# Hybrid attention and mLSTM block: x normalised by tokens and turned on TensorE, GpSimd out of the early stage, another order of group 0 and of the modulation

## Chip, cores and metric

One Trainium2 chip, one core. The metric is the device time of one execution in microseconds (us).

## What is computed

One decoder block on x of 512 tokens by 2048 channels, float32. What matters here is its head:

```
mod = c @ w_ada + b_ada
shift, scale, gate = split(mod, 3)
h = rmsnorm(x, norm_gain) * (1 + scale) + shift
proj = h @ w_in
```

`proj` feeds eight attention heads with three dilated windows, four mLSTM heads behind a causal convolution, and gates; two projections, a merge, an output projection, the gated residual and a last RMSNorm follow. All of that is untouched.

## The kernel before

Every product is made of three float32r matmuls: an operand is cast to a high part (`hi`, on ScalarE, ACT), the rest (`lo`) is subtracted (`split`, L170), and hi x hi, hi x lo and lo x hi are summed in PSUM (`mm3`, L273). So each weight costs a cast and a subtraction before TensorE (PE) can use it.

h is needed with channels on partitions, in 16 tiles of 128 channels by 512 tokens; tile k is called h_k here. x is handed in twice, as it is and turned (`xT`); the early stage loads the turned one. `first_norm` squares its 16 tiles, sums them over channels by matmuls with ones and by additions on VectorE (DVE), and gets 1/rms for all 512 tokens on every partition. Tile k is multiplied by it (`normed`, L387), the first on DVE, the others on GpSimd (POOL). `modulated` (L390) then scales and shifts the tile by the modulation of its channels, splits it and stores it to DRAM for later.

The modulation is a product of c with w_ada, done on DVE: for each column of 128 channels two pieces of 1024 values are multiplied with c and summed (`modulation`, L328, the instruction is at L338). A tile of h needs four pieces (scale and shift), 64 in all. Four lists feed the engines: `loads` gives the order of the DMA issues on SyncE's queue (SP), through rings of 8 buffers (`y`, for the pieces), 3 (`raw`) and 1 (`more`); `stream` is the order in which weights are split, three halves ahead of the matmuls (`step`, L254); `pieces` is the modulation, `modulate(n)` brings it to n pieces; `late` holds evacuations. Every engine runs its instructions in the order in which this Python code issues them, and waits by semaphores.

The early stage takes turns k = 0 to 15. Turn k has one weight unit `ws` of two halves (`first_products`: 18 matmuls on h_k, six accumulators kept in PSUM for all turns), and units of the table TURNS (`extra_products`): ten more output columns of 128, whose sums over k are cut in five groups (GROUPS), each group summed in PSUM and then copied (group 0, ACT) or added (L517, DVE) to a tile in SBUF. The pair (g, n) in TURNS stands for group g and the columns n and n+1. 288 + 480 matmuls of 512 columns are the stage. POOL makes `lo` of the `extra` units and of h (except h_0); DVE makes `lo` of `ws`, the pieces and the additions. The modulation is paced by turns: at the start of turn k, 4(k+1) + 2 pieces are asked for, and over the turn four more.

Of the kernel before, what the change touches and what calls it, by code (L numbers as in the profile page):

```python
# [16 lines left out]
P = 128  # L17
# [87 lines left out]
def block_kernel(ctx: ExitStack, tc, xT, x, c, cst, abias, ada, ws, wu, wv, fgain, out):  # L105
# [72 lines left out]
    stream, loads, pieces, ready, late, tasks, beside = [], [], [], [], [], [], []  # L178
    at = {"load": 0, "split": 0, "half": 0, "piece": 0, "raw": 0, "more": 0, "y": 0}
# [9 lines left out]
    def add(u):  # L189
        stream.append(u)  # L190
        loads.append(u)

    def load_ahead():
        while at["load"] < len(loads):
            u = loads[at["load"]]
            if u.ring == "any":
                u.ring = "raw" if at["raw"] < RAW or "more" not in tags else "more"
            if at[u.ring] == {"raw": RAW, "more": MORE, "y": ADA}[u.ring]:
                if u.ring == "more":
                    u.ring = "any"  # L200
                break
            if u.at_load:
                u.at_load()
            u.raw = S(u.ring)
            dma(u.raw[:, : u.width], u.src)
            at["load"] += 1
            at[u.ring] += 1

    def prepare():
# [9 lines left out]
        else:  # L219
# [6 lines left out]
            if later and u.low is None:  # L226
                normed(later.pop(0), nc.gpsimd)
# [67 lines left out]
    def load_x(n):  # L295
        for _ in range(n):
            t = S("gm")
            dma(t, xT[len(xt)])
            xt.append(t)
# [4 lines left out]
    load_x(4)  # L304
# [4 lines left out]
    load_x(12)  # L309
# [8 lines left out]
    nc.vector.tensor_copy(bmod, cs[:, C_BADA : C_BADA + 3 * KD])  # L318
    nc.vector.tensor_scalar(bmod[:, KD : 2 * KD], bmod[:, KD : 2 * KD], 1.0, None, ALU.add)
# [37 lines left out]

    def first_norm():

        acc = S("w")  # L360
        root = const.tile([P, 1], F32, name="root")
        nc.scalar.activation(root, eps, AF.Sqrt)
        ss = PS("m")
        for k in range(KD):
            sq = acc[:, :512] if k == 0 else S("hb")
            nc.scalar.activation(sq, xt[k], AF.Square)
            if k % 3 == 2 and k < KD - 2:
                nc.tensor.matmul(ss, ones, sq, start=k == 2, stop=False)
            elif k:
                nc.vector.tensor_tensor(acc[:, :512], acc[:, :512], sq, ALU.add)  # L370
        nc.tensor.matmul(ss, ones, acc[:, :512], start=False, stop=True)
        rstd = acc[:, 512:]
        nc.scalar.activation(rstd, ss, AF.Sqrt, bias=eps, scale=1.0 / D)
# [7 lines left out]
        for k in range(1, 4):  # L381
            normed(k, nc.gpsimd)

    rs = []
# [4 lines left out]

    def modulated(k):  # L390
        def f():
# [4 lines left out]
            nc.scalar.activation(xt[k], xt[k], AF.Identity, bias=mods[:, k : k + 1], scale=gs)  # L396
# [1131 lines left out]
```

## Time and profile before

| what | us |
|---|---|
| median of 3 runs (1635.78 to 1636.86) | 1635.82 |
| profiled execution | 1637.23 |
| its span | 1635.4 |
| PE busy, share of the span | 1565.2, 96% |
| DVE busy | 1147.9, 70% |
| ACT busy | 704.6, 43% |
| POOL busy | 139.8, 9% |
| chain that ended last | PE 71%, DVE 13%, issue 6%, ACT 4% |

Busy times are unions over an engine's instructions. In the lines of the trace, L is the line of the kernel, `out<-in` names the tiles with their buffer numbers left out, and the name behind `<-` in brackets or after an idle time is what the engine waited for. PEld, the loading of weights, runs beside PE. A matmul's duration contains its way through the array, so that neighbours overlap; the distance of their starts is their price. POOL's 139.8 us lie nearly all in the first seventh of the span.

### The profile page before, as it was taken

The page shows a single profiled execution, that of the slowest core. Times are in us where ns is not written, and L with a number is a line of the kernel's source. Part 1 is how long each engine was busy: PE and PEld are TensorE (multiplying, and loading weights), DVE is VectorE, ACT ScalarE, POOL GpSimd, SP SyncE. Part 2 cuts the span into 40 slices and gives each one's busy share as a digit, 9 for nine tenths or more (in the row PEclk, how much of TensorE's full clock was granted, in tenths as well). Part 3 has the DMA queues.
Part 4 walks back from the last instruction along what each step waited for, and adds up shares of the span by engine and source line. Part 5 has one row for each costly group of instructions (what it writes and reads, how often), then busy time and mean ns, then how long its engine had stood idle before and what let it go on. Part 6 is the DMA issues. An engine that isn't in the chain of part 4 may idle for free.

```text
span 1635.4 us, 24961 instructions
## 1 busy us (share of the span) xinstructions
PE 1565.2 (96%) x9686; PEld 1388.3 (85%) x9686; DVE 1147.9 (70%) x1933; ACT 704.6 (43%) x1189; POOL 139.8 (9%) x112
## 2 busy tenths in 40 slices
PE   3799899999999999999999999999999999999997
PEld 1576689988888888999999999999999788878887
DVE  6788867667746568888788887888896444474445
ACT  3332344335525434455454454454443843343234
POOL 2665540000000000000000000000000000000000
PEclk7999999999999999999999999999999999999999
DMA  8677735665222344344443444444444654432333
GB/s 313 241 276 273 272 113 168 223 217 179 90 94 74 104 163 159 139 152 130 142 144 124 146 145 137 144 142 132 133 161 149 216 176 137 176 105 95 125 117 129
DMA packets 93879, 260.01 MB, mean 159 GB/s; under 512 B 10424, under 2 KB 14648, under 8 KB 93760
## 3 DMA queue, kind: packets, MB, share of 16 engines
q1 hardware_dynamic: 79928, 233.24, 41.6%
q10 hardware_dynamic: 13832, 25.18, 4.4%
q8 instruction: 76, 1.25, 0.3%
q14 instruction: 43, 0.35, 0.1%
HBM read 229.02 MB, written 29.36 MB: 158 GB/s over the span
## 4 chain that ended last, share of the span: by engine, by line
PE 71%; DVE 13%; issue 6%; ACT 4%; DMA 3%; POOL 1%; SPq 0%; ACTq 0%; DVEq 0%; POOLq 0%
PE ps L280 47%; PE ps L807 23%; DVE y L338 3%; DVE lo L173 2%; ACT sh L172 2%; DVE cs L780 1%; DVE e L822 1%; DVE cs L784 1%; DVE cs L785 1%; DMA raw<-ws 1%; DVE sl L173 1%; DVE al L786 1%; DMA p<-kept 1%; DMA more<-ws 1%; ACT gm L396 1%
## 5 line engine op out<-in xcount | busy, mean ns | idle before, releaser
L173 DVE TENSOR_TENSOR lo<-raw,hi 128x512 fp32r<-128x512 f32 (+2 forms) x238 | 177.5, 751 | 172.1 <-ACT hi L172 171.7
L172 ACT CAST hi<-raw 128x512 fp32r<-128x512 f32 (+3 forms) x276 | 161.2, 596 | 277.9 <-PE ps L280 227.4
L807 PE MATMUL ps<-t,sh 128*128 128x256 f32 x1344 | 245.3, 282 | 0.0
L807 PEld LDWEIGHTS ps<-t,sh 128*128 128x128 f32 x1344 | 208.0, 190 | 0.0
L807 PE MATMUL ps<-t,sl 128*128 128x256 f32 x672 | 189.3, 282 | 0.0
L779 ACT CAST ah<-raw 128x768 fp32r<-128x768 f32 x112 | 93.6, 836 | 204.8 <-issue 105.2
L280 PE MATMUL ps<-ha,hi 128*128 128x512 f32 x384 | 126.5, 409 | 26.1 <-ACT ha L172 17.2
L173 DVE TENSOR_TENSOR sl<-cs,sh 128x1024 fp32r<-128x1024 f32 x112 | 137.3, 1226 | 16.0 <-ACT sh L172 15.7
L172 ACT CAST sh<-cs 128x1024 fp32r<-128x1024 f32 x112 | 117.6, 1050 | 67.8 <-DVE cs L785 67.4
L786 DVE TENSOR_TENSOR al<-raw,ah 128x768 fp32r<-128x768 f32 x112 | 106.9, 955 | 52.8 <-ACT ah L779 52.6
L280 PE MATMUL ps<-hi,h 128*128 128x512 f32 (+1 forms) x512 | 143.6, 366 | 0.0
L280 PE MATMUL ps<-hi,ha 128*128 128x258 f32 (+1 forms) x512 | 129.8, 339 | 0.0
L280 PE MATMUL ps<-hi,hb 128*128 128x258 f32 (+1 forms) x512 | 129.3, 339 | 0.0
L807 PEld LDWEIGHTS ps<-t,sl 128*128 128x128 f32 x672 | 127.8, 190 | 0.0
L280 PE MATMUL ps<-hb,hi 128*128 128x512 f32 x384 | 122.0, 397 | 1.6 <-POOL hb L173 1.6
L280 PEld LDWEIGHTS ps<-ha,hi 128*128 128x128 f32 x384 | 73.9, 195 | 48.3 <-ACT ha L172 19.2
L280 PEld LDWEIGHTS ps<-hi,h 128*128 128x128 f32 x512 | 91.8, 188 | 17.0
L807 PE MATMUL ps<-hb,ah 128*128 128x256 f32 x448 | 87.1, 287 | 11.5 <-DVE e L822 9.9
L280 PEld LDWEIGHTS ps<-hi,ha 128*128 128x128 f32 x512 | 87.8, 188 | 11.4 <-issue 0.4
L280 PEld LDWEIGHTS ps<-hi,hb 128*128 128x128 f32 x512 | 87.9, 188 | 10.8
L280 PE MATMUL ps<-lo,h 128*128 128x512 f32 (+1 forms) x256 | 93.9, 367 | 2.4 <-DVE lo L173 2.4
L280 PE MATMUL ps<-h,hi 128*128 128x512 f32 x286 | 89.6, 395 | 0.0
(276 smaller groups left out, 3461.8 us busy)
## 6 DMA issues: line engine op xcount, KB each, us to landing
raw<-wu SPq DMA_DIRECT2D x223, 512.0 KB, 3.6
y<-ada SPq DMA_DIRECT2D x64, 512.0 KB, 7.3
g<-kept SPq DMA_DIRECT2D x56, 256.0 KB, 3.9
kept<-e ACTq DMA_DIRECT2D x56, 256.0 KB, 2.5
raw<-ada SPq DMA_DIRECT2D x24, 512.0 KB, 3.7
more<-wu SPq DMA_DIRECT2D x16, 512.0 KB, 3.5
raw<-wv SPq DMA_DIRECT2D x12, 516.0 KB, 3.7
kept<-g ACTq DMA_DIRECT2D x20, 256.0 KB, 4.2
```

Of the source, the lines that this page charges most:

```text
L172: nc.scalar.copy(hi, src)
L173: (low or nc.vector).tensor_tensor(lo, src, as32(hi), ALU.subtract)
L280: nc.tensor.matmul(ps, a, b, start=first and n == 0, stop=last and n == 2)
L338: nc.vector.tensor_tensor_reduce(out=raw[:, :1024], in0=raw[:, :1024], in1=cb[half][:, :1024], scale=1.0, scalar=bmod[:, col : col + 1] if ...
L396: nc.scalar.activation(xt[k], xt[k], AF.Identity, bias=mods[:, k : k + 1], scale=gs)
L779: nc.scalar.copy(ah, r[:, HT : 4 * HT])
L780: nc.vector.tensor_tensor(two(s[:, : 2 * HT]), two(r[:, HT : 3 * HT]), r[:, :HT].unsqueeze(1).to_broadcast([P, 2, HT]), ALU.add,)
L784: nc.vector.tensor_tensor(s[:, 2 * HT : 3 * HT], s[:, :HT], r[:, 2 * HT : 3 * HT], ALU.add)
L785: nc.vector.tensor_tensor(s[:, 3 * HT :], s[:, 2 * HT : 3 * HT], r[:, 3 * HT : 4 * HT], ALU.add)
L786: nc.vector.tensor_tensor(al, r[:, HT : 4 * HT], as32(ah), ALU.subtract)
L807: nc.tensor.matmul(banks[bank][:, n * HT : (n + 1) * HT], x[:, w], y, start=count[bank] == 1, stop=count[bank] == 24 * len(BANKS[bank]),)
L822: nc.vector.tensor_tensor(v[:, 0:2, :], twice(v[:, 4, :]), two(bb), ALU.add)
```

## The change

- The turned copy of x is no longer handed in. The early stage loads x with tokens on partitions, 16 tiles of 128 tokens by 512 channels. The squares are summed along the row by the squaring instruction itself (10 tiles on ACT, 6 on DVE), so 1/rms is one value per partition. The tiles are scaled in groups of four (`normed`, on ACT; the first group half on DVE), and turned on PE by `turned`: four matmuls with the identity into one PSUM tile, then a copy by ACT (h_0 is read from PSUM). Tiles 0 to 3 are turned at the start, two more after each of the first six `ws`.
- GpSimd makes no `lo` and no scaling any more; DVE makes every `lo`.
- TURNS puts all five units of group 0 into turn 1.
- `loads` is two lists, one for the `y` ring and one for the others.
- The modulation is paced by matmuls: one piece more per 10 matmuls issued, besides 4(k+1) + 2 at the start of turn k.

The core of the diff (left out: the removed input's plumbing and line-for-line renames of the two lists):

```diff
-    1: [(0, 0)], 2: [(0, 2), (0, 4)], 3: [(0, 6)], 4: [(0, 8)],
+    1: [(0, 0), (0, 2), (0, 4), (0, 6), (0, 8)],
...
-            if later and u.low is None:
-                normed(later.pop(0), nc.gpsimd)
...
+    def load_x(j):
+        for t in range(NT):
+            xn[j][t] = S("gm")
+            dma(xn[j][t], x[t * P : (t + 1) * P, j * T : (j + 1) * T])
...
     def first_norm():
+        sums = const.tile([P, NT, NT], F32, name="sums")
+        for j in range(NT):
+            for t in range(NT):
+                to, junk = sums[:, t, j : j + 1], S("hb")
+                if (j * NT + t) % 8 in (2, 5, 7):
+                    nc.vector.tensor_tensor_reduce(
+                        out=junk, in0=xn[j][t], in1=xn[j][t], scale=1.0, scalar=0.0,
+                        op0=ALU.mult, op1=ALU.add, accum_out=to,
+                    )
+                else:
+                    nc.scalar.activation(junk, xn[j][t], AF.Square, accum_out=to)
...
+        nc.vector.tensor_reduce(rstd, sums, mybir.AxisListType.X, ALU.add)
+        nc.scalar.activation(rstd, rstd, AF.Sqrt, bias=eps, scale=1.0 / D)
         nc.vector.reciprocal(rstd, rstd)
-        normed(0, nc.vector)
+        normed(0, True)
+        for k in range(4):
+            turned(k)
         modulate(3)
         for _ in range(2):
             prepare()
         modulate(4)
-        for k in range(1, 4):
-            normed(k, nc.gpsimd)
+        normed(1)
...
+    def normed(j, both=False):
+        for t in range(NT):
+            r = rstd[:, t : t + 1]
+            if both and t % 2:
+                nc.vector.tensor_scalar(xn[j][t], xn[j][t], r, None, ALU.mult)
+            else:
+                nc.scalar.activation(xn[j][t], xn[j][t], AF.Copy, scale=r)
+
+    def turned(k):
+        ps = PS("m")
+        for t in range(NT):
+            nc.tensor.transpose(ps[:, t * P : (t + 1) * P], xn[k // 4][t][:, k % 4 * P : (k % 4 + 1) * P], ident)
+        if k == 0:
+            xt.append(ps)
+        else:
+            xt.append(S("hb" if k < HK else "gm"))
+            nc.scalar.copy(xt[k], ps)
...
-            split(xt[k], a, b, nc.gpsimd if k else None)
+            split(xt[k], a, b)
...
-    AHEAD = 2
-    def next_pieces():
-        k, n, i = turn
-        modulate(4 * (k + 1) + AHEAD + 4 * (i + 1) // n)
-        turn[2] += 1
+    AHEAD, PACE = 2, 10
+    def next_pieces(n):
+        emitted[0] += n
+        modulate(4 + AHEAD + emitted[0] // PACE)
...
     def first_products(k, half):
+            if half == 1 and k < 6:
+                for i in range(2 * k + 4, 2 * k + 6):
+                    turned(i)
+                if k % 2 == 1 and k < 4:
+                    normed(k // 2 + 2)
...
-            next_pieces()
+            next_pieces(9)
...
-                Unit(next(src)[:, :width], width, [extra_products(g, n), extra_products(g, n + 1)], low=nc.gpsimd)
+                Unit(next(src)[:, :width], width, [extra_products(g, n), extra_products(g, n + 1)])
...
-    loads[:5] = loads[1:4] + loads[:1] + loads[4:5]
+    load_ahead("y", 3)
+    load_ahead("raw", 1)
     load_ahead()
```

How the order moves is shown at the end of turn 4 and the start of turn 5. ACT before, from the last cast of group 0 (`gm_103` is h_4, L515 copies products of group 0 out of PSUM, `raw_498` is the `ws` of turn 5):

```order
L172 CAST hi_597<-raw_467 128x256
L396 ACTIVATE gm_103<-gm_103,mods,gs_621 128x512
L172 CAST ha_624<-gm_103 128x512
L162 DMA kept_627<-gm_103 128x512
L172 CAST hi_629<-raw_498 128x384
L172 CAST hi_643<-raw_498 128x384
L515 COPY g_647<-ps_634 128x512
L172 CAST hi_659<-more_539 128x512
L515 COPY g_663<-ps_649 128x512
```

ACT in the change, from the second half of turn 5's `ws` (`raw_531`) to h_5 (`hb_332`); L409 copies turned tiles out of PSUM, `more_566` is the first `extra` unit of turn 5:

```order
L172 CAST hi_711<-raw_531 128x384
L409 COPY gm_729<-ps_724 128x512
L409 COPY gm_736<-ps_731 128x512
L172 CAST hi_740<-more_566 128x512
L420 ACTIVATE hb_332<-hb_332,mods,gs_749 128x512
L172 CAST ha_752<-hb_332 128x512
```

Copies of turned tiles stand where copies of group 0 stood, and they come right before the cast of `hi_740`, with h_5 behind it.

DVE before, at the same place (the ISA rows are pieces of the modulation with the reading of their sums, `gs` is the last scalar before h is made, `gs_717` that of h_5):

```order
L173 TENSOR_TENSOR lo_644<-raw_498,hi_643 128x384
L338 ISA y_614,mods<-y_614,w_134,acc_641 128x1024
L338 ISA mods 128x1
L338 ISA y_616,acc_697<-y_616,w_133,bmod 128x1024
L338 ISA acc_697 128x1
L338 ISA y_618,mods<-y_618,w_134,acc_697 128x1024
L338 ISA mods 128x1
L393 TENSOR_TENSOR gs_717<-mods,cs 128x1
```

DVE in the change, up to h_5 (`gs_749`):

```order
L173 TENSOR_TENSOR lo_712<-raw_531,hi_711 128x384
L173 TENSOR_TENSOR lo_741<-more_566,hi_740 128x512
L340 ISA y_551,acc_744<-y_551,w_132,bmod 128x1024
L340 ISA acc_744 128x1
L340 ISA y_592,mods<-y_592,w_133,acc_744 128x1024
L340 ISA mods 128x1
L414 TENSOR_TENSOR gs_749<-mods,cs 128x1
L173 TENSOR_TENSOR ha_752<-hb_332,ha_752 128x512
```

A `lo` of an `extra` unit (`lo_741`), which POOL made before, stands ahead of the last two pieces of h_5, and the subtraction of h_5 stands behind them.

PE in the change, the end of turn 4's `ws` and the start of turn 5's (L404 turns x, L281 is the product):

```order
L281 MATMUL ps_295<-ha_688,hi_643 128x512 x2
L281 MATMUL ps_295<-ha_688,lo_644 128x512
L404 MATMUL ps_724<-cs,gm_117 128x128
L404 MATMUL ps_724<-cs,gm_119 128x128
L404 MATMUL ps_724<-cs,gm_121 128x128
L404 MATMUL ps_724<-cs,gm_123 128x128
L404 MATMUL ps_731<-cs,gm_117 128x128
L404 MATMUL ps_731<-cs,gm_119 128x128
L404 MATMUL ps_731<-cs,gm_121 128x128
L404 MATMUL ps_731<-cs,gm_123 128x128
L281 MATMUL ps_290<-ha_752,hi_680 128x512 x2
L281 MATMUL ps_290<-ha_752,lo_681 128x512
```

The eight turns stand between the two `ws`; before, PE had two halves of group 0 there, the last unit of that group.

## Rows read from the trace of the kernel before

**Rows 1.** Busy time by stretch: columns are named in the first line.
```profile
core 0: us, PE busy (x) PEld busy (x) DVE busy (x) ACT busy (x) POOL busy (x), PEclk, DMA share, GB/s
10.00:20.00 10.00, 7.12 (x9) 1.68 (x8) 5.99 (x9) 6.34 (x11) 0.00 (x0) 0.87 1.03 401
...
24.55:36.07 11.52, 0.00 (x1) 0.00 (x1) 9.86 (x13) 1.48 (x3) 7.81 (x4) 0.50 0.80 292
...
36.07:105.20 69.13, 57.88 (x213) 43.02 (x213) 56.33 (x71) 24.54 (x49) 39.60 (x26) 0.91 0.70 253
...
246.77:400.00 153.23, 153.23 (x1044) 141.17 (x1043) 102.93 (x209) 61.33 (x114) 0.00 (x0) 1.00 0.61 204
...
200.00:220.00 20.00, 20.00 (x87) 16.18 (x86) 14.94 (x22) 8.96 (x16) 10.14 (x7) 1.00 0.53 193
```

**Rows 2.** Timeline, DVE, one turn: start us, us, engine, line, operation [idle before <-releaser].
```profile
121.33 0.68 DVE L517 TENSOR_TENSOR g<-g,ps 128x512 f32<-128x512 f32 x1
121.94 1.27 DVE L338 CUSTOM_DVE_ANT_0 y<-y,w,bmod 128x1024 f32<-128x1024 f32 x1
...
126.57 1.33 DVE L173 TENSOR_TENSOR lo<-raw,hi 128x384 fp32r<-128x384 f32 x1 [1.95 <-ACT hi L172]
127.83 2.31 DVE L338 CUSTOM_DVE_ANT_0 y<-y,w,bmod 128x1024 f32<-128x1024 f32 x1
...
212.59 0.15 DVE L393 TENSOR_TENSOR gs<-mods,cs 128x1 f32<-128x1 f32 x1
```

**Rows 3.** Groups by line and shape, 0 to 245 us: busy us, mean ns | idle before.
```profile
L338 DVE CUSTOM_DVE_ANT_0 y<-y,w,bmod 128x1024 f32<-128x1024 f32 x32 | 59.2, 1850 | 0.0
...
L338 DVE CUSTOM_DVE_ANT_0 y<-y,w,acc 128x1024 f32<-128x1024 f32 x32 | 47.7, 1489 | 0.7
...
L173 DVE TENSOR_TENSOR lo<-raw,hi 128x384 fp32r<-128x384 f32 x24 | 31.1, 1302 | 22.1 <-ACT hi L172 22.1
```

**Rows 4.** Timeline, the start, up to the first matmuls on h0.
```profile
8.54 8.03 ACT L366 ACTIVATE hb<-gm 128x512 f32<-128x512 f32 x12 [0.74 <-DMA gm<-xT]
...
24.55 2.29 DVE L338 CUSTOM_DVE_ANT_0 y<-y,w,bmod 128x1024 f32<-128x1024 f32 x1
...
34.37 0.15 DVE L393 TENSOR_TENSOR gs<-mods,cs 128x1 f32<-128x1 f32 x1
...
36.05 0.69 DVE L173 TENSOR_TENSOR ha<-gm,ha 128x512 fp32r<-128x512 f32 x1 [1.53 <-ACT ha L172]
...
36.07 1.52 PE L280 MATMUL ps<-ha,hi 128*128 128x512 f32 x2 [16.27 <-ACT ha L172]
...
36.66 0.55 DVE L173 TENSOR_TENSOR lo<-raw,hi 128x384 fp32r<-128x384 f32 x1
```

**Rows 5.** Timeline, PE, the first matmul behind the early stage.
```profile
246.77 0.28 PE L280 MATMUL ps<-hi,ha 128*128 128x258 f32 x1
```

**Rows 6.** Groups by line and shape over the whole span, for prices.
```profile
L173 DVE TENSOR_TENSOR lo<-raw,hi 128x512 fp32r<-128x512 f32 x190 | 129.7, 688 | 129.6 <-ACT hi L172 129.4
...
L515 ACT COPY g<-ps 128x512 f32<-128x512 f32 x10 | 5.8, 582 | 0.9 <-PE ps L280 0.9
...
L1298 ACT ACTIVATE y<-y,fr 128x512 f32<-128x512 f32 x8 | 5.4, 716 | 0.9 <-DVE fr L1294 0.9
...
L982 PE MATMUL ps<-cs,w 128*128 128x128 f32 x32 | 4.8, 272 | 0.0
```

**Rows 7.** Busy time by stretch, after the two gaps of PE.
```profile
54.72:58.00 3.28, 2.99 (x7) 2.02 (x8) 3.28 (x2) 1.95 (x5) 3.28 (x3) 0.53 0.98 317
66.36:76.00 9.64, 9.64 (x42) 7.82 (x42) 8.57 (x11) 3.66 (x8) 6.50 (x5) 1.00 0.80 290
```

**Rows 8.** Timeline, PE, matmuls behind a gap [idle before <-releaser].
```profile
43.97 0.50 PE L280 MATMUL ps<-ha,hi 128*128 128x512 f32 x1 [0.93 <-ACT ha L172]
...
54.72 0.64 PE L280 MATMUL ps<-ha,hi 128*128 128x512 f32 x1 [2.41 <-ACT hi L172]
...
66.36 0.73 PE L280 MATMUL ps<-ha,hi 128*128 128x512 f32 x2 [2.37 <-ACT g L515]
```

More of the change, by code (lines that the diff above doesn't have):

```diff
@@ L104, in block_kernel @@
 @with_exitstack
-def block_kernel(ctx: ExitStack, tc, xT, x, c, cst, abias, ada, ws, wu, wv, fgain, out):
+def block_kernel(ctx: ExitStack, tc, x, c, cst, abias, ada, ws, wu, wv, fgain, out):
     nc = tc.nc
@@ L177, in block_kernel @@
     pos = [0, 0]
-    stream, loads, pieces, ready, late, tasks, beside = [], [], [], [], [], [], []
-    at = {"load": 0, "split": 0, "half": 0, "piece": 0, "raw": 0, "more": 0, "y": 0}
+    stream, loads, pieces, ready, late, tasks, beside = [], {"y": [], "raw": []}, [], [], [], [], []
+    at = {"split": 0, "half": 0, "piece": 0, "raw": 0, "more": 0, "y": 0}
     def begin(*desc):
@@ L190, in add, with load_ahead @@
         stream.append(u)
[L191 to L207, printed above, removed]
+        loads["raw"].append(u)
+    def load_ahead(only=None, most=99):
+        for kind in [only] if only else loads:
+            while loads[kind] and most:
+                u = loads[kind][0]
+                if u.ring == "any":
+                    u.ring = "raw" if at["raw"] < RAW or "more" not in tags else "more"
+                if at[u.ring] == {"raw": RAW, "more": MORE, "y": ADA}[u.ring]:
+                    if u.ring == "more":
+                        u.ring = "any"
+                    break
+                if u.at_load:
+                    u.at_load()
+                u.raw = S(u.ring)
+                dma(u.raw[:, : u.width], u.src)
+                loads[kind].pop(0)
+                at[u.ring] += 1
+                most -= 1
     def prepare():
@@ L293, in block_kernel @@
     begin_part("heads", "left", y=(8, 1032), w=(4, 1024), gm=(17, 512), mk=(1, P))
[L295 to L299, printed above, removed]
+    xn = [[None] * NT for _ in range(NT)]
+    def load_x(j):
+        for t in range(NT):
+            xn[j][t] = S("gm")
+            dma(xn[j][t], x[t * P : (t + 1) * P, j * T : (j + 1) * T])
     crow = [S("g") for _ in range(4)]
@@ L308, in block_kernel @@
     tri = cs[:, C_TRI : C_TRI + P]
-    load_x(12)
+    for j in range(1, NT):
+        load_x(j)
     mask = S("mk")
@@ L348, in modulation @@
             u = Unit(ada[col * 2 + half], use=use(half), at_load=at_load if half == 0 else None, ring=ring)
-            loads.append(u)
+            loads["y" if ring == "y" else "raw"].append(u)
             (pieces if then or ring == "y" else stream).append(u)
@@ L356, in block_kernel @@
     qm, km, szm = [None] * 8, [None] * 8, [None] * 8
+    rstd = const.tile([P, NT], F32, name="rstd")
     def first_norm():
-        acc = S("w")
         root = const.tile([P, 1], F32, name="root")
         nc.scalar.activation(root, eps, AF.Sqrt)
[L363 to L373, printed above, removed]
+        sums = const.tile([P, NT, NT], F32, name="sums")
[9 more added lines that the diff above has]
+                    nc.scalar.activation(junk, xn[j][t], AF.Square, accum_out=to)
+        nc.vector.tensor_copy(bmod, cs[:, C_BADA : C_BADA + 3 * KD])
+        nc.vector.tensor_scalar(bmod[:, KD : 2 * KD], bmod[:, KD : 2 * KD], 1.0, None, ALU.add)
+        nc.vector.tensor_reduce(rstd, sums, mybir.AxisListType.X, ALU.add)
+        nc.scalar.activation(rstd, rstd, AF.Sqrt, bias=eps, scale=1.0 / D)
         nc.vector.reciprocal(rstd, rstd)
-        rs.append(rstd)
-        normed(0, nc.vector)
+        normed(0, True)
+        for k in range(4):
+            turned(k)
         modulate(3)
@@ L395, in f @@
             )
[L396 removed]
+            src = xt[k]
+            if k == 0:
+                xt[0] = S("hb")
+            nc.scalar.activation(xt[k], src, AF.Identity, bias=mods[:, k : k + 1], scale=gs)
             if k < HK:
@@ L443, in f @@
                 modulate(4 * (k + 1) + AHEAD)
-                turn[:] = [k, 2 * (1 + len(TURNS.get(k, []))), 0]
             if k == 0 and half == 0:
@@ L764, in pair_units @@
                 unit = Unit(src, ring="raw")
-                loads.append(unit)
+                loads["raw"].append(unit)
                 paired.append((d, u, unit))
```

19 lines of the change are left out of this document (5 added, 14 removed).

## The prediction

> **What bounds the kernel now.** I read the stretches first [rows 1], then the order of time on VectorE (DVE) in one turn of the early stage [rows 2], then the groups of instructions by line up to 245 us [rows 3]. The reader should see two kernels in one. From 246.8 us on TensorE (PE) is busy without a gap for the next 153 us and nearly so to the end (1565 us of the whole span), and no line of the change touches that part: what the early stage loses or wins, the end loses or wins. The early stage is 768 matmuls of 512 columns (288 `first`, 480 `extra`). Dense, 87 of them take 20 us, 0.230 us each [rows 1], 176.6 us in all; they stand from 36.07 us [rows 4] to 246.77 us [rows 5], 210.7 us, so PE loses 34 us there. From 24.55 [rows 4] to 212.6 us [rows 2] DVE carries the pieces, and until about 193 us it is the bound: in a turn [rows 2] it runs four pieces of the modulation, two `lo` halves and some additions, and stands idle once, 1.95 us, until ScalarE (ACT) has cast the new h. These idles sum to 22.1 us before the larger `lo` group [rows 3], and to 30 with the rest of the 16 turns. PE waits for that chain at each turn's start.
>
> A piece of 1024 columns takes 1.27 us when GpSimd (POOL) is still and up to 2.31 us when it works, 1.67 in the mean of all 64; a `lo` of 384 columns 1.3 in the mean instead of 0.55 [rows 2 to 4]. So GpSimd's help is paid by DVE.
>
> **The change part by part.** The sum is made against the profiled execution, 1637.2 us with a span of 1635.4; the median of the runs is 1635.8, and I move the result down by 1.4 us at the end. A measurement can tell about 0.2%, 3.3 us, from no change.
>
> *GpSimd out.* The 64 pieces go from 106.9 us [rows 3] to 64 x 1.27 = 81: minus 25. Up to the last piece 29 `lo` of 384 go from 1.3 to 0.5: minus 23. DVE takes over 24 `lo` of 512 at 0.61 (their duration is 0.69 [rows 6], but after an addition of 0.68 the next instruction starts 0.61 later [rows 2]), 10 of 256 at about 0.33 (scaled) and 15 of h at 0.61: plus 27. The idle for h becomes 1.53 us, as at the first h, where DVE already did the subtraction [rows 4], minus 6. DVE's own work from the first piece to the last falls from 188 us (24.55 to 212.6) to about 161. That is the gain the change can reach, if DVE never stands idle in a new place.
>
> *Start.* The squares stay paced by x, whose last square ended at 16.57 us [rows 4]. Matmuls of the sum, a root and a reciprocal over 512 columns, 8 us up to the first piece at 24.55 [rows 4], fall away; 16 sums per row and four small instructions (some 0.2 us each) follow, so rstd stands near 17.8. Two scalings on DVE (an estimate of 0.5 each, under the 0.69 of a subtraction with two operands [rows 6]) end at 18.8, three pieces at 22.6. On ACT two scalings (0.7 [rows 6]) end at 19.2; then PE does 16 turns. A turn of 128x128 costs 0.15 us at full clock [rows 6]; PE stands at half clock here [rows 1], so 0.3 and an end at 23.2. Copy, two casts, two `lo`, the fourth piece: 26.7. From gs to the first matmul 1.7 us passes [rows 4]: **28.4 instead of 36.07**, 7.7 us won. Loads: the activations' matrix pieces go ahead of the second ws, which by the rate of the start (some 400 GB/s [rows 1], 1.3 us per 512 KB) lands near 28.7; it is wanted at 31, so the new load order costs nothing, and that margin is its cover. x comes in as many and as large pieces as before. SP's queue keeps its place otherwise: a y load no longer stands behind a raw load that waits, which takes waits away.
>
> *The turns on PE.* 48 more of 0.15 us lie on PE's path: 7 us. More costly is what hangs behind them, in order, on three queues. After each of the first six ws, PE gets two tiles to turn; ACT's next two instructions copy them out; only behind those copies (and after turns 1 and 3 behind four scalings) stands the cast of the next `hi`; DVE's next instruction waits for that cast, and behind it stand the pieces of the next h. Before, the casts that stood behind copies of PSUM were those whose `lo` POOL made; DVE's own `lo` was cast right behind h.
>
> Let E be the end of the 18 matmuls of a ws. Both tiles are turned at E+1.2 and copied at E+1.9 (0.58 a copy [rows 6]), the cast is done at E+2.5, `lo` at E+3.1, two pieces at E+5.6 (a cast of 512 is put at a copy's 0.6), and gs to PE adds 1.7: the next h is there at **E+7.3**; PE has nothing from E+1.2 on. With four scalings in between (2.7 us) but one piece less behind them it is E+8.4. The 18 matmuls take 4.1 us, or 5.7 when the clock starts at half after such a gap; I take the half start where the gap is over 3 us. PE's starts of h0, h1 and so on then are:
> - h1: E0 = 35.4 (18 matmuls took 7.0 at the start [rows 4, 8]); ACT scales the next group first; copies at 37.4, cast 37.8, `lo`, one piece, gs: **41.0** (before 43.97 [rows 8]).
> - Turn 1 holds all 60 matmuls of group 0: 18 + 60 matmuls, 17.9 us, half a clock at the start 1.6, turns 1.2, a stop of 2 us where the copies and scalings stand before the cast of `hi`, and one of 2 us for the two PSUM buffers left: h2 at **65.8**. DVE stands still for some 7 us there.
> - h3 follows at once: **71.3**. h4, with the scalings: E3 = 75.5, **83.9**. h5: E4 = 89.6, **97.0**.
> - Turn 5 has 48 more matmuls that need no new h, but pieces are now due one per 10 matmuls, and 216 matmuls ask for 27 pieces where h6 needs 28: the 28th is only asked for with h6 itself, after the last addition. E5 = 102.7, turns 1.2, 11.0 of matmuls, addition, piece, gs: **118.4**. At this point the kernel before had also done these 216: its records count 213 from 36.07 to 105.20 us [rows 1]. So 13 us behind.
> - Turns 6 to 8 (42 matmuls, 9.7 us): by the same chain (last addition, piece, gs) 13.4, 11.7 and 10.7 us, since the rule by matmuls gets ahead by one or two pieces per turn: h9 at **154.2** with 342 matmuls done.
> - From there DVE (10.7 us for 42 matmuls) and PE (9.7) run abreast and the pieces end early: 426 x 0.230 = 98.0, plus some 2 us for DVE in turns 11 and 12, plus 2 in the last ten halves, where DVE now does `lo`, addition and convolution (0.33 + 0.6 + 0.7 per 1.38 us of PE). End of the stage: **256**, against 246.8: **9 us later**, 1646 for such an execution and **1645** as a median.
>
> Unknown prices: scaling on ACT lies between a copy's 0.58 and, as far above the like row [rows 6], 0.85; I take that row, 0.7. A turn lies between 0.06, a quarter of a dense 512-column matmul, and 0.27, its whole duration [rows 6]; I take the dense 0.15. The two move the end by minus 5 and plus 6 us. The clock: after a gap of 2.41 us the matmuls ran at about half clock for 3.3 us, after one of 2.37 us at full clock [rows 7, 8], each seen once. If it never falls after h0, the end comes 4.5 us sooner; if it falls at every start to h9, 4 later.
>
> The Trainium skill (TensorE: Matmul & The Clock Gate, section Loop structure matters more than you think) holds that long waits between groups of matmuls let the array go cold and the next ones run slow. This case's trace agrees at one of the two gaps and not at the other. By that rule the sum would be the one of a fall at every start, 1649; by the gap that kept its clock, 1640.5.
>
> **The rivals.** *DVE's relief wins.* For it: DVE was idle at no other place than h, so 27 us of work less could come through whole. Then the pieces end at 18.8 + 161.5 + 2 = 182, PE then has some 165 matmuls left after the next `lo` (2.8 us), 38 us, with PE's own work in turn 1 and the tail 4 to 8 more: 229, 18 us sooner, **1618**. It decides if DVE waits for the copies of the turns for less than 1 us per turn. Against it: the cast of `hi` stands behind the copies by the order. The Trainium skill (SBUF — State Buffer, section Who interferes with whom) has a VectorE instruction with two SBUF inputs and a GpSimd instruction that reads SBUF contend for a shared pair of ports. The trace agrees, 1.27 against 2.31 us [rows 2], and this rule alone would give this rival. *Half of it:* waits on ACT and PE overlap better than I add them, and the start's 7.7 us cover them: **1634 to 1639**, no change. *Worse:* the half clock holds through the turns to h6, and DVE's casts miss each turn by an addition more: 10 us on top, **1655**.
>
> **How the numbers follow.** My sum adds many waits in series; an error of 8 us in it is easy, and it can lose more than it can gain. Forecast (9 us slower, itself 1639 to 1651): 0.52; worse: 0.10; no change: 0.13; relief wins, whole or in good part: 0.25. Faster 0.25, same 0.13, slower 0.62. The range leaves out the far half of the relief and of the worse case: **1622 to 1654**.
>
> **What would show it.** Right: the first matmul near 28; DVE idle several us before a `lo` in turns 1 to 5, released by an ACT cast that itself waited for copies of PSUM; PE gaps of 3 to 7 us before h4, h5 and h6; 216 matmuls at about 118 us; pieces of 1.27 us; dense PE from about 155. Wrong: fewer than 15 us of such idles on DVE, or 216 matmuls done by 105 us; then the relief wins.

## The result, and the profile after

The changed kernel takes 1659.77 us (median of 4 runs, 1658.78 to 1660.82), the kernel before in runs on the same chip 1636.34 us: a ratio of 1.0143, 95% interval 1.0125 to 1.016. It is 23.4 us slower. The forecast had the sign, but it said 9 us where the runs show 23, and its range ended at 1654.

| | before | after |
|---|---|---|
| profiled execution, its span | 1637.23, 1635.4 | 1660.09, 1657.8 |
| first matmul on h0 | 36.07 [rows 4] | 28.00 |
| end of the early stage (first 128x258 matmul) | 246.77 [rows 5] | 264.13 |
| from there to the end | 1388.6 | 1393.7 |
| busy: PE, DVE, ACT, POOL | 1565.2, 1147.9, 704.6, 139.8 | 1578.7, 1127.1, 719.0, 17.6 |

PE's timeline after, at the starts of h0, h1 and h4 to h9 and at the end of the stage (columns as in [rows 2], which answers for DVE; the two lines of L404 are the turns behind the 18 matmuls on h4 and on h5):

```profile
28.00 1.52 PE L281 MATMUL ps<-ha,hi 128*128 128x512 f32 x2 [5.00 <-ACT ha L172]
...
40.04 1.52 PE L281 MATMUL ps<-ha,hi 128*128 128x512 f32 x2 [4.26 <-ACT ha L172]
...
81.38 1.52 PE L281 MATMUL ps<-ha,hi 128*128 128x512 f32 x2 [6.94 <-ACT ha L172]
...
88.69 1.03 PE L404 MATMUL ps<-cs,gm 128*128 128x128 f32 x8
95.79 1.52 PE L281 MATMUL ps<-ha,hi 128*128 128x512 f32 x2 [6.07 <-ACT ha L172]
...
102.76 1.03 PE L404 MATMUL ps<-cs,gm 128*128 128x128 f32 x8
...
118.99 1.52 PE L281 MATMUL ps<-ha,hi 128*128 128x512 f32 x2 [3.55 <-ACT ha L172]
...
135.54 1.52 PE L281 MATMUL ps<-ha,hi 128*128 128x512 f32 x2 [3.55 <-ACT ha L172]
...
149.31 0.51 PE L281 MATMUL ps<-hb,hi 128*128 128x512 f32 x1 [2.10 <-ACT hb L172]
...
160.58 0.50 PE L281 MATMUL ps<-hb,hi 128*128 128x512 f32 x1 [0.77 <-ACT hb L172]
...
264.13 0.28 PE L281 MATMUL ps<-hi,ha 128*128 128x258 f32 x1
```

PE starts 8 us earlier than before [rows 4] and still ends the stage 17 us later: the gaps in brackets, from h1 on, are PE waiting for an h. DVE is not short of speed. Its groups by line and shape up to 271 us answer to [rows 3]:

```profile
L340 DVE CUSTOM_DVE_ANT_0 y<-y,w,acc 128x1024 f32<-128x1024 f32 x32 | 41.0, 1280 | 0.5
L340 DVE CUSTOM_DVE_ANT_0 y<-y,w,bmod 128x1024 f32<-128x1024 f32 x32 | 40.9, 1278 | 0.0
...
L173 DVE TENSOR_TENSOR lo<-raw,hi 128x384 fp32r<-128x384 f32 x24 | 13.2, 554 | 12.0 <-ACT hi L172 12.0
```

The 64 pieces fell from 106.9 to 81.9 us and the larger `lo` from 1302 to 554 ns, as forecast. What DVE does before h4 shows where the time goes. First DVE's timeline after, then ACT's:

```profile
72.67 1.28 DVE L340 CUSTOM_DVE_ANT_0 y<-y,w,bmod 128x1024 f32<-128x1024 f32 x1
...
78.00 0.56 DVE L173 TENSOR_TENSOR lo<-raw,hi 128x384 fp32r<-128x384 f32 x1 [4.05 <-ACT hi L172]
78.47 1.28 DVE L340 CUSTOM_DVE_ANT_0 y<-y,w,acc 128x1024 f32<-128x1024 f32 x1
...
79.68 0.15 DVE L414 TENSOR_TENSOR gs<-mods,cs 128x1 f32<-128x1 f32 x1
81.36 0.69 DVE L173 TENSOR_TENSOR ha<-hb,ha 128x512 fp32r<-128x512 f32 x1 [1.53 <-ACT ha L172]
```

```profile
74.05 1.07 ACT L409 COPY gm<-ps 128x512 f32<-128x512 f32 x2 [3.15 <-PE ps L404]
75.00 2.56 ACT L398 ACTIVATE gm<-gm,rstd 128x512 f32<-128x512 f32 x4
77.46 0.50 ACT L172 CAST hi<-raw 128x384 fp32r<-128x384 f32 x1
```

DVE stands still for 4.05 us in front of a `lo`, whose cast stands behind two copies and four scalings. Behind that `lo` comes the last of the four pieces of h4, then `gs`, then h4. Two readings were possible: the cast comes too late (the order on ACT, which the forecast blamed), or the piece stands on the wrong side of the `lo` (the pacing).

### The profile page after: what moved, and what is told of

Read it like the earlier page. It is cut to its first block, busy times and chain, and to the rows that moved or that the text cites. A ratio compares the mean times of both kernels' runs of the same rounds, so it can differ in the third digit from the quotient of the medians.

```text
span 1657.8 us, 25089 instructions
## 1 busy us (share of the span) xinstructions
PE 1578.7 (95%) x9740; PEld 1407.0 (85%) x9740; DVE 1127.1 (68%) x2001; ACT 719.0 (43%) x1222; POOL 17.6 (1%) x32
## 4 chain that ended last, share of the span: by engine, by line
PE 78%; DVE 9%; DMA 5%; ACT 4%; issue 3%; SPq 0%; ACTq 0%; DVEq 0%
PE ps L281 50%; PE ps L833 27%; DVE y L340 2%; DVE lo L173 1%; ACT sh L172 1%; DMA p<-kept 1%; DMA gm<-x 1%; DVE cs L806 1%; DMA y<-ada 1%; DVE e L848 1%; DVE sl L173 1%; DMA g<-kept 1%; DVE cs L810 0%; DVE cs L811 0%; DVE h L173 0%
## 5 line engine op out<-in xcount | busy, mean ns | idle before, releaser
L173 DVE TENSOR_TENSOR lo<-raw,hi 128x512 fp32r<-128x512 f32 (+3 forms) x276 | 181.5, 662 | 170.4 <-ACT hi L172 170.0
L281 PE MATMUL ps<-ha,hi 128*128 128x512 f32 x384 | 133.4, 429 | 32.8 <-ACT ha L172 29.4
L812 DVE TENSOR_TENSOR al<-raw,ah 128x768 fp32r<-128x768 f32 x112 | 106.9, 954 | 54.1 <-ACT ah L805 53.7
L281 PE MATMUL ps<-hi,h 128*128 128x512 f32 (+1 forms) x512 | 143.6, 366 | 0.0
L281 PE MATMUL ps<-hi,ha 128*128 128x258 f32 (+1 forms) x512 | 129.8, 339 | 0.0
L281 PE MATMUL ps<-hi,hb 128*128 128x258 f32 (+1 forms) x512 | 129.2, 339 | 0.0
L281 PE MATMUL ps<-hb,hi 128*128 128x512 f32 x384 | 121.4, 396 | 5.1 <-ACT hb L172 2.9
L281 PEld LDWEIGHTS ps<-ha,hi 128*128 128x128 f32 x384 | 77.4, 205 | 56.9 <-ACT ha L172 31.3
L281 PEld LDWEIGHTS ps<-hi,h 128*128 128x128 f32 x512 | 91.8, 188 | 17.0
L281 PEld LDWEIGHTS ps<-hi,ha 128*128 128x128 f32 x512 | 87.9, 188 | 11.4 <-issue 0.4
L281 PEld LDWEIGHTS ps<-hi,hb 128*128 128x128 f32 x512 | 87.9, 188 | 10.9
L281 PE MATMUL ps<-lo,h 128*128 128x512 f32 (+1 forms) x256 | 93.9, 367 | 2.4 <-DVE lo L173 2.4
L281 PEld LDWEIGHTS ps<-hb,hi 128*128 128x128 f32 x384 | 71.5, 188 | 23.5 <-ACT hb L172 3.7
```

The costliest lines, as they stand in the source:

```text
L173: (low or nc.vector).tensor_tensor(lo, src, as32(hi), ALU.subtract)
L281: nc.tensor.matmul(ps, a, b, start=first and n == 0, stop=last and n == 2)
L812: nc.vector.tensor_tensor(al, r[:, HT : 4 * HT], as32(ah), ALU.subtract)
```

## The experiments

Each kernel ran beside runs of the kernel before, whose medians were 1635.5 to 1636.7 us; ratios are to those. "Stage" is the first 128x258 matmul, "behind" the rest of the span.

**Four single edits of the changed kernel.** The order on ACT:

```diff
-                    turned(i)
+                    late.append(lambda i=i: turned(i))
...
-                    normed(k // 2 + 2)
+                    late.append(lambda: normed(k // 2 + 2))
```

> The copies of the turned tiles and the scalings of the next group of x are issued behind the cast of the next hi instead of ahead of it. Theory (the wait of DVE's lo for a cast that stands behind copies of PSUM is what the early stage loses): ACT copies 2 x 0.6 us less ahead of the cast in turns 0 to 5 and four scalings (2.4 us) less in two of them, some 8 to 12 us in all; the waits of DVE's lo for ACT's hi fall from 41 us to under 30; the first 128x258 matmul at 252 to 256 us instead of 264.1, the median at 1648 to 1652. Rival 1 (DVE's added work is the cost): DVE's work is the same, so no change, 1658 to 1661. Rival 2 (PE's time for the 64 turns of x is the cost): no change either.

Measured: 1652.43 us (1.0099, 1.0084 to 1.0114), stage 255.96; the waits of DVE's `lo` for ACT's `hi` in the first 271 us fell from 39.1 to 29.9 us. The median came as the theory had it, but it takes back only 7 of the 23 us.

```diff
-    AHEAD, PACE = 2, 10
+    AHEAD, PACE = 6, 10
```

> Every piece of the modulation is asked for four pieces earlier (AHEAD 6 instead of 2), everything else kept. Theory (pieces are asked for too late, the last one of an h only behind the last addition): the gaps of PE at h6 to h9 close, turns 6 to 8 take 10 to 11 us each instead of 16.5, 14.5 and 11.3; matmul 427 starts near 152 instead of 161 us, the stage ends 6 to 10 us sooner, median 1650 to 1654; the gaps of 3.55 us go and with them the half clock behind them. Rival 1 (DVE's work is the bound there): pieces in another order are the same work, the gaps move to other places and the stage ends within 2 us of 264. Rival 3 (the casts behind the copies alone): turns 6 to 8 have no copies, so no change there.

Measured: 1633.5 us (0.9981, 0.9972 to 0.9991), stage 238.53. Three times what was expected: 26 us, all of the loss and a little more, from nothing but asking four pieces earlier. So rival 1 falls: the same DVE work ends 26 us sooner. And the pacing was at work before h6, not in turns 6 to 8 alone: h5 starts at 80.72 instead of 95.79 us. DVE still stands idle for 4.06 us in front of a `lo` in this run, but it does so a turn ahead: the last piece of h5 stands behind that `lo`, where it was the last piece of h4, and PE waits 1.90 us for h5 instead of 6.07. DVE's timeline of this run, then PE's:

```profile
77.34 0.56 DVE L173 TENSOR_TENSOR lo<-raw,hi 128x384 fp32r<-128x384 f32 x1 [4.06 <-ACT hi L172]
```

```profile
80.72 0.49 PE L281 MATMUL ps<-ha,hi 128*128 128x512 f32 x1 [1.90 <-ACT ha L172]
```

```diff
-    1: [(0, 0), (0, 2), (0, 4), (0, 6), (0, 8)],
+    1: [(0, 0)], 2: [(0, 2), (0, 4)], 3: [(0, 6)], 4: [(0, 8)],
```

> Group 0's second products lie in turns 1 to 4 as in the kernel before, the rest of the change is kept. Theory: the 60 matmuls of turn 1 fill no wait, since h2's pieces stand behind them; spread, 48 of them fill PE's waits at h3, h4 and h5 (13, 12, 14 us for 18 matmuls of 4.1 us now) while h2 comes some 10 us sooner: h6 at 108 to 113 instead of 119 us, median 1648 to 1654. Rival 1 (DVE's work up to h6 is the bound): the same pieces, lo and additions lie ahead of h6, so h6 stays at 117 to 120 and the median within 2 us of 1660.

Measured: 1670.98 us (1.021, 1.0189 to 1.023), stage 277.07: it is 11 us slower, and both expectations missed. The rule counts matmuls: with 48 of them moved to later turns, the pieces are asked for later still (15, 18 and 21 at the ends of turns 2 to 4, not 17, 19 and 21).

```diff
-  [extra_products(g, n), extra_products(g, n + 1)])
+  [extra_products(g, n), extra_products(g, n + 1)], low=nc.gpsimd)
```

> The lo halves of the extras go back to GpSimd; everything else of the change is kept. Rival 1 (DVE's added work is the cost): DVE loses some 34 lo (24 x 0.61 and 10 x 0.33, 18 us) and the stage ends 8 to 18 us sooner, 1642 to 1652. Theory (chain of casts behind copies, pieces asked for too late; GpSimd's help is paid by DVE): pieces go from 1.28 to some 1.6 us wherever GpSimd works and the waits for the casts stay, so the stage ends between 4 us sooner and 10 us later, 1656 to 1670.

Measured: 1654.48 us (1.0113, 1.0098 to 1.0128), stage 260.19. This lies between the two expectations: DVE's pieces went up to 1625 and 1419 ns (from 1278 and 1280), and GpSimd's queue took over waits that had held DVE. It tells little of the cause: the 5 us gained are what DVE was spared less what the slower pieces cost, and the run does not part the two.

**The pacing alone.** The changed kernel with the pacing of before:

```diff
-    AHEAD, PACE = 2, 10
-    emitted = [0]
+    turn = []
+    AHEAD = 2
...
-        emitted[0] += n
-        modulate(4 + AHEAD + emitted[0] // PACE)
+        k, n, i = turn
+        modulate(4 * (k + 1) + AHEAD + 4 * (i + 1) // n)
+        turn[2] += 1
```

> The changed kernel with the pacing of before: within turn k the pieces asked for rise from 4(k+1)+2 to 4(k+2)+2, whatever the number of matmuls; everything else of the change is kept. Theory as it stands after the last runs (the rule by matmuls asks too late: at the ends of turns 2 to 5 it has asked for 17, 19, 21 and 27 pieces, the rule by turns for 18, 22, 26 and 30): most of what four pieces earlier gave comes back, stage end at 238 to 246 us instead of 264.1, median 1633 to 1641. Rival (the casts behind the copies are the larger part): stage end at 252 to 260, median 1648 to 1656. Rival 1 (DVE's added work): within 2 us of 1660.

Measured: 1626.11 us (0.994, 0.9921 to 0.9959), stage 231.33. That is better than the theory's 1633 to 1641. Without its pacing the change is 10 us **faster** than the kernel before; the pacing costs the changed kernel 33.7 us. DVE's timeline of this run, in the same turn as above:

```profile
70.10 0.56 DVE L173 TENSOR_TENSOR lo<-raw,hi 128x384 fp32r<-128x384 f32 x1
70.57 1.28 DVE L340 CUSTOM_DVE_ANT_0 y<-y,w,bmod 128x1024 f32<-128x1024 f32 x1
...
71.89 1.28 DVE L340 CUSTOM_DVE_ANT_0 y<-y,w,acc 128x1024 f32<-128x1024 f32 x1
...
73.11 0.15 DVE L414 TENSOR_TENSOR gs<-mods,cs 128x1 f32<-128x1 f32 x1
74.79 0.69 DVE L173 TENSOR_TENSOR ha<-hb,ha 128x512 fp32r<-128x512 f32 x1 [1.53 <-ACT ha L172]
```

Both last pieces of h4 stand here where the changed kernel's DVE stood still, and `gs` of h4 comes at 73.11 instead of 79.68 us. The copies and scalings on ACT are still there. PE's waits in the stage say the same; first the changed kernel (20 to 271 us), then this run (20 to 245 us; columns: us, times, longest):

```profile
PE ps L281 <- ACT ha L172: 29.4, 6, 6.9
```

```profile
PE ps L281 <- ACT ha L172: 11.4, 4, 5.0
```

The same rule in the kernel before, nothing else changed:

```diff
-        modulate(4 * (k + 1) + AHEAD + 4 * (i + 1) // n)
+        modulate(4 + AHEAD + emitted[0] // PACE)
```

> The kernel before with nothing but the new pacing (4 + 2 + one piece per 10 matmuls instead of by turns). Theory (the rule by matmuls is the cost, whoever normalises and turns x): at the ends of turns 2 to 5 it has asked for 15, 18, 21 and 27 pieces against 18, 22, 26 and 30, so the pieces of h3 to h6 come only with their own turn: stage end 15 to 35 us later than 246.8, median 1651 to 1671. Rival (the rule hurts only together with the turned tiles and their copies): median within 5 us of 1636.

Measured: 1686.38 us (1.0303, 1.0286 to 1.0321), stage 298.73, behind 1388.6: 50 us slower, where no tile of x is turned on PE. The rule is a loss by itself, larger than the expected 15 to 35 us. With group 0 spread it costs the changed kernel about as much (1670.98 us above, 1624.11 us with the pacing by turns below, 47 us): putting group 0 into turn 1, which brings the matmuls forward that the rule counts, hides some 13 us of it. PE's waits from 20 to 300 us there:

```profile
PE ps L280 <- ACT ha L172: 37.6, 8, 16.3
PE ps L280 <- POOL ha L173: 9.7, 7, 1.6
```

**Do the edits add?** The first two single edits together, then with the third:

> Four pieces earlier and the casts ahead of the copies, both. Alone they took 26 and 7 us off the changed kernel. Theory that each removes a wait of its own: both come through, stage end near 231, median 1626 to 1628. Rival (they shorten the same waits of PE for h): stage end at 236 to 240, median 1631 to 1635.

Measured: 1632.49 us (0.9979, 0.9968 to 0.999), stage 236.94. The rival came true: it is 1 us less than with early pieces alone, which the intervals do not part from nothing. A late cast costs little where DVE has pieces to run meanwhile.

> Four pieces earlier, casts ahead of the copies, and group 0's second products spread over turns 1 to 4. Theory that spreading hurt alone (1671) only because the rule by matmuls then asked for pieces still later: with pieces four ahead the 48 matmuls fill waits of PE at h3 to h5, so 2 to 6 us below the kernel with the first two edits alone. Rival (turn 1 with all 60 is the better place, since DVE works ahead meanwhile): 2 us or more above it.

Measured: 1629.97 us (0.9965, 0.9955 to 0.9976), stage 235.67: it is 2.5 us better. Spreading group 0, which cost 11 us under the rule by matmuls, helps once pieces come early. The same two edits on top of the pacing by turns, one each:

> The changed kernel with the pacing by turns and with the casts of hi ahead of the copies and scalings. Theory (with pieces in time the copies ahead of the casts cost little, since DVE has pieces to run meanwhile): median 1622 to 1627, that is 0 to 4 us under the pacing by turns alone (1626.1). Rival (the order on ACT is a loss of its own, 6 turns by 1 to 2 us): 1615 to 1621.

> The changed kernel with the pacing by turns and with group 0's second products in turns 1 to 4 as before: what is left is x's normalisation and turning. Theory that group 0 in one turn leaves turns 2 to 4 without work to fill PE's waits (2.5 and 1.6 us at h4 and h5 in the last trace): 1 to 5 us faster than 1626.1. Rival (in turn 1 the 60 matmuls give DVE 14 us to run ahead, and that is worth more): 2 us or more slower.

Measured: 1624.03 us (0.9923, 0.991 to 0.9935), stage 229.68, and 1624.11 us (0.9923, 0.9911 to 0.9936), stage 229.89. Both are as expected, 2 us each. Their intervals overlap with that of the pacing by turns alone (0.9921 to 0.9959); the stages end 1.7 and 1.4 us sooner in the profiled executions. So what the forecast took for the cause, the cast behind the copies, is worth 7 us under the late pacing and about 2 without it.

**DVE's relief alone.** The kernel before, GpSimd left with the scaling only:

```diff
-            split(xt[k], a, b, nc.gpsimd if k else None)
+            split(xt[k], a, b)
...
-  [extra_products(g, n), extra_products(g, n + 1)], low=nc.gpsimd)
+  [extra_products(g, n), extra_products(g, n + 1)])
```

> The kernel before, in which DVE instead of GpSimd makes the lo halves of h and of the extras; GpSimd only scales x; no turns of x on PE, the old pacing and order. Rival 1 (DVE's added work is the cost): 24 + 10 + 15 lo more on DVE, 27 us, of which less than half comes back from faster pieces: stage end 8 to 15 us later than 246.8, median 1644 to 1651. Theory (GpSimd's help is paid by DVE; the loss lies in pacing and in the order on ACT): pieces go from 1.67 to some 1.4 us and lo of 384 from 1.3 to below 0.9, 30 us less, so the stage ends between 10 us sooner and 3 us later, median 1626 to 1639.

Measured: 1634.92 us (0.9993, 0.998 to 1.0006), stage 243.6. This is no difference that can be told, and it is in the theory's range: the pieces took 1406 and 1390 ns, and what DVE gained there paid for the `lo` it took over.

**The part behind the early stage.** It takes 1393.7 instead of 1388.6 us, though no line of it was changed. In the pair stage (the 128x256 matmuls, from about 645 to 1262 us before) a matmul lasts a constant 283 ns after, and lasted 277 ns at least and 281 in the median before. The same group of matmuls before, then after, 740 to 1240 us (shortest, median and longest in ns); the granted clock there is 1.00 in both:

```profile
L807 PE MATMUL ps<-t,sh x1086: 277/281/416, 740.1 to 1239.9; 128*128 128x256 f32 x181
```

```profile
L833 PE MATMUL ps<-t,sh x1080: 283/283/283, 741.5 to 1239.5; 128*128 128x256 f32 x180
```

The change adds two small constant tiles, 96 bytes per partition (the program rounds each tile up to a multiple of 32). Tiles are laid out from two sides of SBUF, the memory on the chip that the engines work on, and the large tiles of the left side, which lie behind the constant ones, move by that: the remainder of their byte address divided by 128 goes from 32 to 0 ("modulo 128" below). The operand `t` of the pair stage, which streams through the array, is among them; `sh` and `sl`, which are loaded as weights, lie on the right side, at 0 in all kernels.

```diff
-        root = const.tile([P, 1], F32, name="root")
-        nc.scalar.activation(root, eps, AF.Sqrt)
+        nc.scalar.activation(rstd[:, :1], eps, AF.Sqrt)
```

> The changed kernel with the pacing by turns and one small constant tile less, so that the tiles of the left side, the stationary operands t of the pair stage among them, lie 32 bytes off a multiple of 64 as in the kernel before; in the changed kernel they lie on multiples of 64, as sh and sl do in both. Theory (the address makes the constant 283 ns of the pair stage's matmuls, 281 in the mean before, and with it most of the 4.4 us that the part behind the early stage takes longer): the durations alternate again, the part behind takes 1389 to 1390 instead of 1393.0 us, median 1621 to 1624. Rival (something else in the program): 283 ns stays, median 1625 to 1628.

Measured: 1622.08 us (0.991, 0.9896 to 0.9924), behind 1387.9 instead of 1393.0. The median is in the theory's range, and the part behind is even 1 us shorter (but `t` is the operand that streams, not the stationary one as the expectation has it, and the address went to 96, not back to 32). The control in the kernel before:

```diff
+    const.tile([P, 1], F32, name="pad")
```

> The kernel before with one unused small constant tile of 32 bytes, which moves the tiles of its left side onto multiples of 64 and changes nothing else. Theory of the addresses: the pair stage's matmuls take a constant 283 ns instead of 281 in the mean, and the part behind the early stage some 1393 instead of 1388.6 us: median 1639 to 1641. Rival (the difference was in the changed program, not in the addresses): 1634 to 1637, durations alternate as before.

Measured: 1627.19 us (0.9952, 0.994 to 0.9964), stage 246.61, behind 1377.6: 8.8 us **faster**, against both expectations. An unused tile of 32 bytes moves the whole kernel by half a per cent. The address does decide, but modulo 128: this is 64, which no kernel had so far. The edit of the shifted run in the changed kernel itself, and then the three gains on top of each other:

> The changed kernel itself, pacing by matmuls kept, with one small constant tile less, so that the left side's tiles lie 32 bytes off a multiple of 64 as before the change. Theory of the addresses: the part behind the early stage 1388 to 1390 instead of 1393.7 us, the early stage as it was: median 1654 to 1656. Rival: 1658 to 1661.

> The changed kernel with the pacing by turns, the casts of hi ahead of the copies, group 0's second products spread over turns 1 to 4, and the shifted addresses. Alone on top of the pacing by turns they gave 2.1, 2.0 and 4.0 us. If they add: 1617 to 1619. Rival (order on ACT and spreading shorten the same waits of PE at h4 and h5): 1620 to 1622.

Measured: 1656.37 us (1.0129, 1.0116 to 1.0142), stage 265.96, behind 1388.1; and 1618.98 us (0.9899, 0.9885 to 0.9913), stage 228.65, behind 1388.1. In the changed kernel itself the part behind is 1388.1 as expected, while the stage ended 1.8 us later than in the changed kernel, so that the median is just above the theory's range; and the gains add. Last, both at 64:

```diff
-        sums = const.tile([P, NT, NT], F32, name="sums")
+        sums = ssq[:, :, :NT]
```

> The changed kernel, its pacing by matmuls kept; the 16 sums of squares lie in a constant tile that is used again at the end, so the left side's tiles lie at 64 modulo 128 instead of 0. Theory (addresses modulo 128 set the pair stage's matmuls: 283 ns at 0, 281 at 32 and 96, 278 at 64): early stage as it was, the part behind it 1377 to 1379 instead of 1393.7 us, median 1642 to 1646. Rival (the kernel before gained by something else): 1655 to 1661.

> The kernel with all gains of the early stage (pacing by turns, casts of hi first, group 0 spread), its left side at 64 modulo 128. Theory: early stage ends near 228.7 as at 96 modulo 128, the part behind takes 1377 to 1379, median 1606 to 1610. Rival: 1617 to 1620, as at 96.

Measured: 1649.55 us (1.0084, 1.0069 to 1.01), stage 266.38, behind 1380.9; and **1612.97 us (0.9858, 0.9842 to 0.9874)**, stage 228.29, behind 1382.9: the fastest version, 1.4% under the kernel before. Both miss the theory's ranges, by 3.6 and 3.0 us: they gain 7 and 6 us from 96 to 64, and the part behind takes 1380.9 and 1382.9 us where the theory said 1377 to 1379, as in the kernel before at 64 (1377.6). The pair stage by address, from its first to its last 128x256 matmul:

| modulo 128 | kernels | pair stage, us |
|---|---|---|
| 0 | changed; pacing by turns; that with cast first (all ten kernels at 0: 617.7 to 619.7) | 618.5, 619.2, 619.3 |
| 32 | before; its pacing by matmuls; its `lo` on DVE | 616.5, 615.7, 617.6 |
| 96 | the three shifted ones | 613.5, 614.2, 613.7 |
| 64 | before; changed; all gains | 606.4, 606.6, 608.6 |

Groups by line and shape, 740 to 1240 us: the changed kernel (0), the kernel before (32), the same with the unused tile (64).

```profile
L833 PE MATMUL ps<-t,sh 128*128 128x256 f32 x1080 | 198.3, 283 | 0.0
...
L833 PE MATMUL ps<-hb,ah 128*128 128x256 f32 x360 | 70.8, 289 | 5.1 <-DVE e L848 4.8
```

```profile
L807 PE MATMUL ps<-t,sh 128*128 128x256 f32 x1086 | 197.7, 282 | 0.0
...
L807 PE MATMUL ps<-hb,ah 128*128 128x256 f32 x360 | 70.0, 287 | 8.5 <-DVE e L822 7.2
```

```profile
L808 PE MATMUL ps<-t,sh 128*128 128x256 f32 x1101 | 193.5, 278 | 0.0
...
L808 PE MATMUL ps<-hb,ah 128*128 128x256 f32 x368 | 70.5, 285 | 14.9 <-DVE e L823 14.7
```

Between 0 and 32 the ranges touch (617.7 and 617.6), so that difference is the least certain of the four. The mean falls from 283 to 278 ns, and PE begins to wait for DVE's `e` (5, 8.5, 15 us in these 500 us): at 64 the faster matmuls run into the next bound. The granted clock from 740 to 1240 us is 1.00 in all three, so it is not the clock. Why the address counts, and which pair of tiles meets, was not tried.

## Why the forecast was right in sign and wrong in size

**Right, or within 2.5 us.** The first matmul (28.4 forecast, 28.00), the pieces at 1.27 us, h1 (41.0; 40.04), h2 (65.8; 64.18), h3 (71.3; 69.16), h4 (83.9; 81.38), h5 (97.0; 95.79), h6 with 216 matmuls done (118.4; 118.99), the gaps of 3.5 to 7 us before h4 to h6, the idles of DVE in front of a `lo`. That h6 came out within 0.6 us is in part luck: up to h4 the terms were 2.5 us too long in sum, and from h4 to h6 they were 3.1 us too short. Of these, 2.9 us are one term: the 18 matmuls behind a long gap "take 4.1 us, or 5.7 when the clock starts at half", and they took 7.3 us at h4 (81.38 to 88.69) and 7.0 at h5 (95.79 to 102.76), because the granted clock stayed at 0.50, that is 1.2 GHz, for most of them.

**The steps that failed.** From the forecast's 1645.0 to 1659.8 there are 14.8 us, which these terms make up but for rounding:
- "Turns 6 to 8 (42 matmuls, 9.7 us): ... 13.4, 11.7 and 10.7 us": they took 16.55, 13.77 and 11.27, plus 5.8. The text takes the half clock "where the gap is over 3 us", forecasts such gaps before h6 and h7 by its own chain, and then reckons turns 6 and 7 at full clock. The busy times by stretch, columns as in [rows 1], show the clock at half behind h4, h5, h6 and h7:

```profile
81.38:84.70 3.32, 3.32 (x7) 2.40 (x8) 3.28 (x6) 0.36 (x1) 0.00 (x0) 0.50 0.73 227
84.70:87.70 3.00, 3.00 (x8) 2.32 (x8) 0.35 (x1) 0.00 (x0) 0.00 (x0) 0.51 0.86 283
95.79:99.10 3.31, 3.31 (x7) 2.39 (x8) 3.27 (x6) 0.47 (x1) 0.00 (x0) 0.50 0.80 239
99.10:101.30 2.20, 2.20 (x6) 1.70 (x6) 0.50 (x1) 0.00 (x0) 0.00 (x0) 0.50 0.82 259
119.00:122.30 3.30, 3.30 (x7) 2.38 (x8) 3.26 (x6) 0.45 (x1) 0.00 (x0) 0.50 0.72 225
122.30:125.00 2.70, 2.70 (x8) 2.02 (x8) 1.05 (x2) 0.51 (x1) 0.00 (x0) 0.50 0.91 299
128.00:131.90 3.90, 3.90 (x18) 2.91 (x16) 2.49 (x4) 0.62 (x1) 0.00 (x0) 1.00 0.35 101
135.50:138.80 3.30, 3.26 (x7) 2.36 (x8) 3.24 (x6) 0.51 (x1) 0.00 (x0) 0.50 0.67 230
```

  In turn 6 the first 14 matmuls took 6.35 us (118.99 to 125.34), where 0.230 us each make 3.2; in turn 7 the first 8 took 3.62 (135.54 to 139.16), where it would be 1.8. That is 3.1 and 1.8 us, 4.9 of the 5.8; the cause of the other 0.9 us stays open.
- h6 was 0.6 late, and the remaining 426 matmuls took 103.6 us (160.58 to 264.13), 1.6 more than the 102 of the text.
- "What the early stage loses or wins, the end loses or wins": the part behind took 5.1 us more. 2.0 lie in the pair stage; the addresses move that stage by up to 12 us, but no run compares 32 and 0 within one kernel, so that these 2.0 are the address is likely and not shown. 3.0 lie behind the pair stage, 2.0 of them in one wait of PE for ACT at 1298 us (2.7 instead of 0.7 us). This last part took 372.6 to 374.2 us in every kernel built on the one before and 374.5 to 376.5 in every changed one, at any address; the fastest version has no such wait and still takes 375.5. Its cause stays open.
- 1.6 us are the time around the span (2.3 instead of 1.8) and the shift to the median (0.3 instead of 1.4).

**The reason given.** The sum walked the pieces where the new rule puts them ("`lo` at E+3.1, two pieces at E+5.6") and so came out near, but it put the loss down to the copies ahead of the cast, and spoke of the pacing only from h6 on. The runs turn that round: the pacing is 33.7 us, the cast 2 to 7. So the forecast's sum held the right waits, and its account of what makes them was wrong. Nowhere did the text ask what the old pacing would have done in the same chain; by turns, the last pieces of h4 wait for no cast, as DVE's timeline of that run shows.

**The rivals.** "DVE's relief wins" had 1618 and a stage of 229 us. With the pacing by turns the changed kernel has 231.33: this rival describes the change without its pacing, copies and all, and its deciding point (waits for copies under 1 us per turn) was the wrong one. "Half of it" (1634 to 1639) is near what pieces asked for four earlier give, 1633.5, and not this change. "Worse", 1655, had the half clock hold through the turns to h6: at h4 and h5 it did hold for most of the 18 matmuls, 2.9 us in all, which the terms before h4, 2.5 us too long, hid; and it came again at h6 and h7.

**The clock.** The starts behind the gaps of 6.94, 6.07, 3.55 and 3.55 us at h4 to h7 ran at a granted clock of 0.50. The Trainium skill (TensorE: Matmul & The Clock Gate, section Loop structure matters more than you think) holds that long waits between matmuls let the array go cold, so that the next ones run slow; the trace agrees at these four gaps (behind another of 3.55 us, in the last section, the clock fell late).

## What to carry over

A prefetch rule that counts another engine's instructions is only as early as those instructions: before changing such a counter, list how many pieces each rule has asked for at the end of every turn, and look for the queue in which a late one stands behind a wait. A wait that ends last need not be the one to remove; work that could run in front of it may be cheaper to move. Where a change adds or removes even small tiles, compare the time of untouched stages, and try the address before explaining them.

## What was not expected of the hardware

- The address modulo 128 of a matmul's SBUF operand: 618 to 620 us for the pair stage at 0, 606 to 609 at 64. In the kernel before, a tile that nobody reads was enough to move it by 10 us.
- The clock behind a gap. In the kernel with group 0 spread, four matmuls behind a gap of 3.55 us still ran at full clock, and only then it fell (busy times by stretch):

```profile
129.80:131.20 1.40, 1.13 (x4) 0.73 (x5) 1.39 (x2) 0.50 (x1) 0.00 (x0) 1.00 0.87 313
131.20:133.00 1.80, 1.80 (x7) 1.38 (x5) 1.76 (x5) 0.00 (x0) 0.00 (x0) 0.57 0.65 182
```

  In the run with the pacing by turns the stretches behind gaps of 2.40 and 2.48 us also began at full clock and had 0.75 and 0.77 in the mean, that behind 1.55 us 1.00. In the changed kernel, two gaps of the same 3.55 us were followed by half clock for some 6 us and for some 3.3 us. So a fall can follow a gap late, it can last for different times, and the length of the gap alone does not tell it.
